# Where matmul operands begin in SBUF: two groups of tiles moved by 96 and 64 bytes

## The chip, the cores and the metric

The kernel runs on one core of a Trainium2 chip. The metric is the device time of one execution in microseconds (us): 1058.58 us, the median of three runs (1058.28 to 1059.94), before the change. A core has TensorE (PE; its weight loads are shown apart as PEld), VectorE (DVE), ScalarE (ACT), GpSimd (POOL) and SyncE (SP), which work side by side and wait for each other by semaphores. SBUF is the on-chip memory; a tile takes the same range of bytes in each of 128 partitions, so "address" here means the byte offset in a partition, and "phase" means that offset modulo 256.

## The reference

One layer of an encoder block on a stream of 1040 rows (16 learned meta rows and 1024 of the input) and 1024 columns, all in float32:

```python
u = rms_norm(h, pre_w)
rq, rk, rv, rg, aq, ak, av, ag, gr, ga = split(u @ w_in)
y_r = (group_norm(retention_fwd(rq, rk, rv) + retention_bwd(rq, rk, rv)) * ret_nw * silu(rg)) @ w_rb
y_a = (windowed_sink_attention(aq, ak, av) * silu(ag)) @ w_ab
out = (sigmoid(gr) * y_r + sigmoid(ga) * y_a) @ w_o
return h + rms_norm(out, post_w)          # meta rows dropped
```

Retention has 4 heads and chunks of 128 rows; attention has 8 query heads, 2 key heads, and sees 128 rows to either side, the meta rows and a sink.

## The kernel before

**Precision.** Each float32 operand of a matmul is split into a high part in the type float32r and the low rest, and a product is three matmuls, in `mm3` (lines 74 to 76): high by high, low by high, high by low. In `nc.tensor.matmul(o, ah, bh)` the second argument is the stationary operand, loaded as weights (128 x 128), and the third is the moving one, whose columns (mostly 512 or 256) stream past. Lines 74 and 75 move the same high part past two sets of weights, line 76 moves the low part. ScalarE or GpSimd makes the high part (`pool_hi`, line 87), VectorE the low one (`dve_lo`, line 90).

**Stages.** Up to about 26 us the input is loaded, scaled and split into `big`, four tiles of 4 x 1040 columns that stay in place; the rows of each are 4160 bytes long. Up to 290 us follow the four retention heads (`retention`), up to 580 us attention (`attention`), both with projections between them (`proj` with `big` as the moving operand, `projT` with `big` as the stationary one). From there on come four products in the manner of Strassen's method (`Phase`, named z for the gates, r and a for the two branches, o for the output): the weight blocks are summed and split into stationary operands `lh` and `ll`, and the right operands are either quarters of the stream, kept in the tiles `big`, or sums of quarters, `T1` in `big` and `T2`, `T3`, `T4` in tiles of their own ("T" in the groups of the profile). Each product is four rows k of `mm3` with 512 columns. The order of the instructions on each engine comes from a planner that works on the program as it is written, with some orders given by hand (`follow`, `issue_after`).

**Where tiles lie.** Tile pools are stacked in SBUF from the left (from low addresses up) or from the right (`side="right"`, from the top down); SBUF is full to within 32 bytes. The right-hand pools are `wp` (weights `wh`, `wl`, and `xm`), `aw` (split queries `aqh`, `aql`, and `raw`), and, in the place of `aw` and `wp` once attention is done, `lp` (`lh`, `ll`, raw weights, sums). The pools on the left are `keep` (small vectors first, then `big`), `ra`, the retention's and attention's own, and in their place at the end `yp`, `gp`, and `yt`, which holds `T2` to `T4`. The program as built places them so:

| tiles | role in matmuls | phase before |
|---|---|---|
| `big`, row k of 4 | moving, in `projT` stationary | 0, 64, 128, 192, by row and column |
| `T2`, `T3`, `T4` | moving | 64 |
| `lh`, `ll`, `wh`, `wl`, `weh`, `aqh` | stationary (`wh`, `wl` moving in `projT`) | 224 |
| retention's and attention's own operands | both | 192 |

The lines that the change touches: `nsink` (line 94, the negated sink logits, read in attention), `mhalf` (line 99, a vector of -0.5, the exponent of `pow` on GpSimd in lines 382, 602 and 1297), and `ms1` in `square` (line 1290 on), a column of 4 bytes per block of output rows, one of four buffers in the pool `gp`, below `yt`.

Of the kernel before, what the change touches and what calls it, by code (L numbers as in the profile page):

```python
# [7 lines left out]
F32 = mybir.dt.float32  # L8
# [8 lines left out]
P = 128  # L17
# [21 lines left out]
def block_kernel(ctx: ExitStack, tc: tile.TileContext, x0, xT, x, meta, w_in, w_rb, w_ab, w_out, post_w,  # L39
# [2 lines left out]
    PSUM = bass.MemoryType.PSUM  # L42

    keep = ctx.enter_context(tc.tile_pool(name="keep", bufs=1))
    w_stack = ExitStack()
    wp = w_stack.enter_context(tc.tile_pool(name="wp", bufs=1, side="right"))
    ps = ctx.enter_context(tc.tile_pool(name="ps", bufs=1, reuse_waits="tile", space=PSUM))
# [43 lines left out]


    vec = keep.tile([P, 2 * KT], F32, name="vec")
    nsink = keep.tile([P, 8], F32, name="nsink")
    dtab = keep.tile([P, 28], F32, name="dtab")
    rcol = keep.tile([P, 9], F32, name="rcol")
    rbc = keep.tile([P, T], F32, name="rbc")
    rnw = keep.tile([P, KT], F32, name="rnw")
    mhalf = keep.tile([P, 16], F32, name="mhalf")
    nc.vector.memset(mhalf, -0.5)  # L100

    def fetch_w(src, u):
# [163 lines left out]
    with tc.tile_pool(name="setup", bufs=1, reuse_waits="tile") as st:  # L266
# [89 lines left out]
        for c in range(9):  # L356
            a, b = cols(c)
            t = st.tile([P, D if c < 7 else T], F32, tag="xn" if c < 7 else "xr", bufs=7 if c < 7 else KT - 1,
                        name=f"xn{c}")[:, 0:D]
# [553 lines left out]
    def gtile(name):  # L913
        return gp.tile([P, 512], F32, tag="g", bufs=6, name=name)
# [347 lines left out]
    def o_post(u, i, j, o, to=None):  # L1262
        if not rows:
            o_head()
        r = 2 * (u ^ 2) + i
        s = slice(512 * j, 512 * j + 512)
        if r not in rows:
            rows[r] = (gp.tile([P, 3], F32, tag="ms2", bufs=4, name=f"ms2_{r}"), [], [])
            if u == 3:
                xres[i] = (lp if i else keep).tile([P, 4, 256], F32, tag="wr", bufs=2, name=f"xres{i}")  # L1270
                xres[i] = xres[i].rearrange("p a b -> p (a b)")
                nc.sync.dma_start(xres[i], x[P * r:P * r + P])
        m2, parts, _ = rows[r]
        square(r, m2, j, o)
        to = o if to is None else to
        if u == 3:

            if not i:
                nc.vector.tensor_tensor(to, o, pw[:, s], mul)
            o = xres[i]  # L1280
        parts.append((s, to, o))
        if len(parts) == 2:
            o_out(r)

    def square(r, m2, c, o):
        m1 = rows[r][2]
        jk = gtile(f"jk{r}_{c}")
        nc.scalar.activation(jk[:, 0:o.shape[1]], o, AF.Square, accum_out=m2[:, c:c + 1])
        if not m1:
            m1.append(gp.tile([P, 1], F32, tag="ms1", bufs=4, name=f"ms1_{r}"))  # L1290
            nc.vector.tensor_scalar(m1[0], m2[:, c:c + 1], 0.25 / D, EPS, op0=ALU.mult, op1=ALU.add)
        else:
            nc.vector.scalar_tensor_tensor(m1[0], m2[:, c:c + 1], 0.25 / D, m1[0], op0=ALU.mult, op1=ALU.add)
# [12 lines left out]
    def o_tail(o, a):  # L1306
        m2, parts, _ = rows[3]
        s = slice(a, a + 256)
        square(3, m2, 2 * (a // 256), o[:, s])
        scaled = nc.vector.tensor_tensor(o[:, s], o[:, s], pw[:, s], mul).ins  # L1310
        if a:
            with tc.issue_after(scaled):
                for c, t, _ in parts:
                    nc.vector.tensor_tensor(t, t, pw[:, c], mul)  # L1314
            parts.append((slice(0, 512), o, xres[1]))
            o_out(3)
# [229 lines left out]
    yp, gp, yt = (ctx.enter_context(tc.tile_pool(name=n, bufs=1, reuse_waits="tile")) for n in ("yp", "gp", "yt"))  # L1546
# [84 lines left out]
```

## Time and profile before

| | |
|---|---|
| median of three runs | 1058.58 us (1058.28 to 1059.94) |
| profiled execution, first to last instruction | 1057.8 us |
| TensorE busy | 1047.6 us, 5880 matmuls |
| weight loads busy | 906.6 us |
| VectorE, ScalarE, GpSimd busy | 839.3, 507.2, 229.0 us |
| moved by DMA | 188.43 MB |

The profiled execution's span is 0.8 us below the median of the runs: that much lies around it. Matmuls are pipelined: the duration that the profile gives of one (about 395 ns at 512 columns) overlaps the next, so the busy share of TensorE says only that it has work; how fast it goes is read from start to start. In rows that list single instructions the columns are start and duration in us, engine, line, operation, names of out<-in, rows * columns of the array and the form.

### The profile page before, as it was taken

What the parts mean: (1) busy time and instruction counts of PE and PEld (TensorE: products, weight loads), DVE (VectorE), ACT (ScalarE), POOL (GpSimd) and SP (SyncE); (2) the same over time, 40 slices, a digit from 0 to 9 for tenths busy, and PEclk for the clock granted to TensorE, in tenths of its full rate; (3) what the DMA queues carried; (4) which work ended last, traced back from release to release, by engine and by line L of the source; (5) the groups of instructions that cost most, each with busy time, mean ns of one, the idle gap of its engine ahead of it and who ended that gap; (6) DMA issues with size and microseconds to landing.
All of it is one profiled execution on the core that took longest, in us unless ns stands there. A gap on an engine that the chain in (4) does not pass through costs nothing. (4 is left out here: it accounts for less than half of the span.)

```text
span 1057.8 us, 17223 instructions
## 1 busy us (share of the span) xinstructions
PE 1047.6 (99%) x5880; PEld 906.6 (86%) x5880; DVE 839.3 (79%) x1788; ACT 507.2 (48%) x1127; POOL 229.0 (22%) x338
## 2 busy tenths in 40 slices
PE   9999999999999999999999999999999999999997
PEld 8998999989989888988888888787888888788886
DVE  7876758768875777778769988998799799778665
ACT  5531422523524566655667554455556446334432
POOL 3345244243242332444310000000000000111032
PEclk9999999999999999999999999999999999999999
DMA  9433222242231466665549679999925746789463
GB/s 352 168 86 86 70 42 80 71 98 89 84 83 61 101 181 192 165 181 159 165 155 338 201 254 321 302 309 353 387 94 168 250 159 232 225 226 317 119 120 79
DMA packets 96758, 188.43 MB, mean 178 GB/s; under 512 B 10944, under 2 KB 35552, under 8 KB 95856
## 3 DMA queue, kind: packets, MB, share of 16 engines
q1 hardware_dynamic: 79120, 162.89, 45.6%
q0 software_dynamic: 10176, 14.73, 9.2%
q10 hardware_dynamic: 7376, 9.73, 2.6%
q8 instruction: 46, 0.75, 0.3%
q14 instruction: 40, 0.33, 0.1%
HBM read 124.32 MB, written 57.68 MB: 172 GB/s over the span
## 5 line engine op out<-in xcount | busy, mean ns | idle before, releaser
L1246 POOL DMA_DIRECT2D mx_d<-c1a x4 | 3.6, 891 | 401.6 <-DVE c1a L1237 382.4
L75 PE MATMUL bz<-T,llz 128*128 128x512 f32 x192 | 75.9, 395 | 0.0
L76 PE MATMUL bz<-T,lhz 128*128 128x512 f32 x192 | 75.7, 394 | 0.0
L74 PE MATMUL bz<-T,lhz 128*128 128x512 f32 x192 | 75.6, 396 | 0.0
L74 PE MATMUL pv<-wh,big 128*128 128x256 f32 x256 | 73.3, 286 | 0.0
L75 PE MATMUL pv<-wh,big 128*128 128x256 f32 x256 | 73.3, 286 | 0.0
L76 PE MATMUL pv<-wl,big 128*128 128x256 f32 x256 | 73.2, 286 | 0.0
L75 PE MATMUL bz<-big,llz 128*128 128x512 f32 x176 | 69.6, 395 | 0.2 <-DVE llz L90 0.2
L76 PE MATMUL bz<-big,lhz 128*128 128x512 f32 x176 | 69.5, 395 | 0.0
L74 PE MATMUL bz<-big,lhz 128*128 128x512 f32 x176 | 68.7, 395 | 0.5 <-ACT lhz L942 0.5
L1377 ACT ACTIVATE p<-raw,nm 128x401 f32<-128x401 f32 (+1 forms) x64 | 38.4, 601 | 33.7 <-DVE nm L1374 32.4
L1387 POOL TENSOR_SCALAR p<-p,den 128x400 f32<-128x400 f32 (+1 forms) x60 | 37.8, 687 | 68.2 <-DVE den L1380 64.1
L74 PE MATMUL paq<-big,wh 128*128 128x512 f32 x128 | 51.8, 405 | 0.0
L75 PE MATMUL paq<-big,wl 128*128 128x512 f32 x128 | 50.7, 396 | 0.0
L76 PE MATMUL paq<-big,wh 128*128 128x512 f32 x128 | 50.5, 395 | 0.0
L75 PEld LDWEIGHTS pv<-wh,big 128*128 128x128 f32 x256 | 48.3, 189 | 0.4
L74 PEld LDWEIGHTS pv<-wh,big 128*128 128x128 f32 x256 | 48.2, 188 | 0.4
L76 PEld LDWEIGHTS pv<-wl,big 128*128 128x128 f32 x256 | 48.3, 189 | 0.3
L76 PEld LDWEIGHTS bz<-T,lhz 128*128 128x128 f32 x192 | 36.0, 188 | 8.9
L75 PEld LDWEIGHTS bz<-T,llz 128*128 128x128 f32 x192 | 36.0, 188 | 8.8 <-DVE llz L90 0.3
L74 PEld LDWEIGHTS bz<-T,lhz 128*128 128x128 f32 x192 | 36.0, 188 | 8.7
L90 DVE TENSOR_TENSOR wl<-wr,wh 128x1024 fp32r<-128x1024 f32 x28 | 34.8, 1247 | 10.8 <-POOL wh L87 6.7
(616 smaller groups left out, 3613.6 us busy)
## 6 DMA issues: line engine op xcount, KB each, us to landing
wrz<-in_w_in_dram SPq DMA_DIRECT2D x32, 512.0 KB, 6.2
wr<-in_w_in_dram SPq DMA_DIRECT2D x29, 512.0 KB, 4.0
we<-in_w_in_dram SPq DMA_DIRECT2D x16, 512.0 KB, 4.2
tg<-tg_d SPq DMA_DIRECT2D x32, 256.0 KB, 5.0
T<-preT SPq DMA_DIRECT2D x6, 1024.0 KB, 8.2
e<-e ACTq DMA_DIRECT2D x20, 256.0 KB, 2.6
e<-e SPq DMA_DIRECT2D x20, 256.0 KB, 4.6
xn<-in_x_dram SPq DMA_DIRECT2D x8, 512.0 KB, 9.2
```

Of the source, the lines that this page charges most:

```text
L74: nc.tensor.matmul(o, ah, bh, start=first, stop=False, **kw)
L75: nc.tensor.matmul(o, al, bh, start=False, stop=False, **kw)
L76: latest[:] = [nc.tensor.matmul(o, ah, bl, start=False, stop=last, **kw).ins]
L90: return nc.vector.tensor_tensor(o, i, hi.bitcast(F32), ALU.subtract).ins
L1246: nc.gpsimd.dma_start(d, to, accum_op=ALU.add)
L1377: last["exp"] = nc.scalar.activation(p[:, 0:1 + wid], raw[e_][:, 0:1 + wid], AF.Exp, scale=-1.0, bias=nm_[:, e_:e_ + 1], accum_out=den[:, ...
L1387: nc.gpsimd.tensor_scalar(pt[e_][:, 0:wid], pt[e_][:, 0:wid], den[:, e_:e_ + 1], 1.0, op0=ALU.mult, op1=ALU.mult)
```

## The change

`nsink` leaves the left-hand pool `keep` for a new right-hand pool `edge`, opened before all others on that side, where it takes 24 columns (96 bytes) of which 8 are used: all other right-hand tiles move down by 96 bytes. `mhalf` grows from 16 to 24 columns, which gives back the 32 bytes that `nsink` took, so that `big` and all behind it stay where they were; four small vectors ahead of it (and `mhalf` itself) move by 32 bytes. `ms1` gets six buffers instead of four, each of which takes 32 bytes: `yt` behind it moves up by 64 bytes. In the program as built, the phase of `T2` to `T4` goes from 64 to 128 and that of `wh`, `wl`, `weh`, `xm`, `aqh`, `aql`, `lh`, `ll`, and the other tiles of `lp` from 224 to 128; `raw` goes from 32 and 128 to 192 and 32. `big` and the operands of retention and attention in left-hand pools keep their addresses. The instructions on every engine and their order are the same; one wait of GpSimd in front of the last `pow` on an `ms1` is gone, and the fill of `mhalf` is longer.

```diff
     keep = ctx.enter_context(tc.tile_pool(name="keep", bufs=1))
+    edge = ctx.enter_context(tc.tile_pool(name="edge", bufs=1, side="right"))
     w_stack = ExitStack()
...
-    nsink = keep.tile([P, 8], F32, name="nsink")
+    nsink = edge.tile([P, 24], F32, name="nsink")[:, 0:8]
...
-    mhalf = keep.tile([P, 16], F32, name="mhalf")
+    mhalf = keep.tile([P, 24], F32, name="mhalf")
     nc.vector.memset(mhalf, -0.5)
...
         if not m1:
-            m1.append(gp.tile([P, 1], F32, tag="ms1", bufs=4, name=f"ms1_{r}"))
+            m1.append(gp.tile([P, 1], F32, tag="ms1", bufs=6, name=f"ms1_{r}"))
```

## The prediction

> **What bounds the kernel.** I read the page first, then the busy time by stage, then the waits of TensorE, and last single matmuls in order of time.
>
> ```profile
> span 1057.8 us, 17223 instructions
> ...
> PE 1047.6 (99%) x5880; PEld 906.6 (86%) x5880; DVE 839.3 (79%) x1788; ACT 507.2 (48%) x1127; POOL 229.0 (22%) x338
> ...
> PEclk9999999999999999999999999999999999999999
> ...
> DVE u3o L1300 0%; DVEq L1627 0%; DVE c5o L1314 0%
> ```
>
> The chain that ended last is not followed back far enough to say anything. The busy shares do: TensorE is at 99% for the whole span, at an undiminished clock. The stages (us, then busy time and count per engine) say it more sharply:
>
> ```profile
> 700.00:870.00 170.00, 170.00 (x731) 136.77 (x730) 152.25 (x250) 90.59 (x161) 0.00 (x0) 1.00 0.70 244
> ...
> 965.00:1057.80 92.80, 86.24 (x383) 69.91 (x381) 60.01 (x112) 34.92 (x74) 18.18 (x22) 0.99 0.54 138
> ```
>
> From 700 to 870 us TensorE has no gap at all; 729 matmuls of 512 columns begin there (two of the 731 began before), 170.00 / 729 = 233.2 ns from start to start. In the last stage only the tail behind the last matmul is without TensorE work (92.80 - 86.24 = 6.6 us). So the time is a number of matmuls times the interval between their starts. The waits of TensorE agree; these are the two longest:
>
> ```profile
> PE idle L309 <- DVE warm L207: 1.5, 1, 1.5
> PE bz L74 <- ACT lhz L942: 0.5, 1, 0.5
> ```
>
> After the 1.5 us at the start nothing that the trace shows keeps TensorE waiting for more than 0.5 us. What a matmul saves, the kernel saves; what it loses, the kernel loses.
>
> **Do the intervals hang on addresses?** The rows of `big` are 4160 bytes long, 64 more than a multiple of 256, so the four rows k of one product start at four different phases (byte address modulo 256). Here is one product from `big` (start, busy, engine, line, tiles), the first of the three matmuls of each k:
>
> ```profile
> 782.48 0.39 PE L74 MATMUL bz<-big,lhz 128*128 128x512 f32 x1
> ...
> 783.17 0.40 PE L74 MATMUL bz<-big,lhz 128*128 128x512 f32 x1
> ...
> 783.88 0.39 PE L74 MATMUL bz<-big,lhz 128*128 128x512 f32 x1
> ...
> 784.57 0.39 PE L74 MATMUL bz<-big,lhz 128*128 128x512 f32 x1
> ...
> 785.27 0.39 PE L74 MATMUL bz<-big,lhz 128*128 128x512 f32 x1
> ```
>
> The moving operand starts at phase 128, 192, 0 and 64 in turn, and three matmuls take 0.69, 0.71, 0.69 and 0.70 us. Two products on a summed block `T`, always at phase 64:
>
> ```profile
> 788.05 0.40 PE L74 MATMUL bz<-T,lhz 128*128 128x512 f32 x1
> 788.29 0.39 PE L75 MATMUL bz<-T,llz 128*128 128x512 f32 x1
> ...
> 793.42 0.39 PE L76 MATMUL bz<-T,lhz 128*128 128x512 f32 x1
> 793.65 0.39 PE L74 MATMUL bz<-big,lhz 128*128 128x512 f32 x1
> ```
>
> 24 matmuls in 5.60 us: 233.3 ns each, 0.700 us for three. Taking the differences of successive starts over the whole trace (those under 250 ns, so that waits are out), with the stationary operand at phase 224, gives for `big`: 232.0 ns at phase 0 (466 intervals), 232.4 at 64 (457), 231.4 at 128 (457), 234.5 at 192 (466); for `T`: 233.4 (992). Where these lie, by the answers on the tile `big` (minimum, median and maximum of one duration, first and last start), its two largest groups of first matmuls with 512 columns:
>
> ```profile
> L74 PE MATMUL bz<-big,lhz x176: 391/394/497, 556.7 to 818.6; 128*128 128x512 f32 x176
> ...
> L74 PE MATMUL paq<-big,wh x128: 388/394/484, 292.9 to 505.0; 128*128 128x512 f32 x128
> ```
>
> and of the tile `T`:
>
> ```profile
> L74 PE MATMUL bz<-T,lhz x192: 389/396/402, 580.3 to 810.2; 128*128 128x512 f32 x192
> ...
> L74 PE MATMUL bo<-T,lho x52: 279/394/403, 978.4 to 1050.7; 128*128 128x512 f32 x44, 128*128 128x256 f32 x8
> ...
> L74 PE MATMUL br<-T,lhr x48: 392/394/403, 827.2 to 888.5; 128*128 128x512 f32 x48
> ...
> L74 PE MATMUL ba<-T,lha x48: 394/396/402, 905.5 to 972.3; 128*128 128x512 f32 x48
> ```
>
> So phase 128 is the cheapest of the four for the moving operand, and the dearest is only 3.1 ns above it.
>
> **The change part by part.** No instruction is added, removed or reordered on any engine; only addresses differ, a fill is 24 columns instead of 16, and one wait on GpSimd is dropped.
>
> *1. Moving operand of the T products, 64 to 128.* From the rows above, (192 + 48 + 48 + 44) x 3 = 996 matmuls of 512 columns. The same step within `big` saves 232.4 - 231.4 = 1.0 ns; from T's own 233.4 to 231.4 it would be 2.0. I take the middle, 1.5 ns, since T shares with the row at 64 the phase and differs in repeating it: 996 x 1.5 = -1.5 us. Ends: 2.0 ns saved (-2.0 us), or 1.1 lost, if 128 beside the new stationary phase costs what the row at 192 costs, 234.5 (+1.1 us).
>
> *2. Stationary operand, 224 to 128.* Phase 224 is 32 bytes off a multiple of 64, 128 is not. The trace has few 512-column intervals in which the weights for the next matmul lie at a multiple of 64: where such a matmul stands ahead of retention or attention. The first and the last of 39:
>
> ```profile
> 81.59 0.39 PE L76 MATMUL pq<-big,wh 128*128 128x512 f32 x1
> 81.83 0.28 PE L74 MATMUL pa<-vh,sh 128*128 128x256 f32 x1
> ...
> 560.21 0.40 PE L74 MATMUL bz<-big,lhz 128*128 128x512 f32 x1
> 560.44 0.28 PE L76 MATMUL po<-pal,vah 128*128 128x256 f32 x1
> ```
>
> Their means are 231.1 (moving phase 0, 8 intervals), 231.8 (64, 16), 232.8 (128, 8) and 233.3 (192, 7): against the means above -0.9, -0.6, +1.4 and -1.2 ns, together -0.3. I take that for all matmuls of 512 columns whose stationary operand moves, 996 with `T` and 1920 with `big`: to the groups of 176 and 128 above come, among the groups by shape,
>
> ```profile
> L74 PE MATMUL pe<-big,weh 128*128 128x512 f32 x80 | 32.0, 404 | 0.0
> ...
> L74 PE MATMUL bo<-big,lho 128*128 128x512 f32 x64 | 25.2, 394 | 0.0
> L74 PE MATMUL br<-big,lhr 128*128 128x512 f32 x64 | 24.9, 394 | 0.0
> L74 PE MATMUL ba<-big,lha 128*128 128x512 f32 x64 | 24.9, 394 | 0.0
> ...
> L74 PE MATMUL pq<-big,wh 128*128 128x512 f32 x48 | 19.0, 395 | 0.0
> ...
> L74 PE MATMUL pq<-big,w 128*128 128x512 f32 x16 | 6.7, 430 | 0.1
> ```
>
> which makes 640 groups of three. 2916 x -0.3 = -0.9 us. Ends are the two extremes: -1.2 ns, so -3.5 us, and +1.4 ns, so +4.1 us. This is the widest term, from the thinnest rows.
>
> [...]
>
> *3. Matmuls of 256 columns.* In projT the moving weights go from 224 to 128 (960 matmuls), in proj the stationary ones (432). The trace has all pairings but the old one with both off 64: moving off and stationary on a multiple of 64 118.7 ns (900 intervals), the reverse 118.4 (486), both on it 118.5 (679). These lie within 0.3 ns: 960 x -0.1 + 432 x 0.1, about -0.1 us. Ends +-0.4 us (1392 x 0.3).
>
> *4. The rest.*
>
> ```profile
> 0.80 0.07 DVE L100 MEMSET mhalf<- 128x16 f32 x1 [0.80 <-PEq L1621]
> ```
>
> is the fill in order of time, and of the line that uses `ms1`:
>
> ```profile
> L1297 POOL TENSOR_TENSOR ms<-ms,mhalf x8: 560/739/1542, 1005.8 to 1052.7; 128x1 f32<-128x1 f32 x8
> ...
>   DVE ms L1293: 54.0, 6
> ```
>
> The longer fill costs between nothing and 0.04 us (half of 0.07 more), ahead of the warm-up matmuls that TensorE waits 1.5 us for and that no result needs: zero. The wait dropped on GpSimd is on one of four `ms1` buffers used again; GpSimd stands idle there until VectorE has made the value (54.0 us in six waits), so a buffer freed earlier ends nothing: zero. VectorE, ScalarE and DMAs write the moved tiles; were they slower by an address, TensorE's waits above leave them room.
>
> Sum: -1.5 - 0.9 - 0.1 = -2.5 us. The profiled execution has a span of 1057.8 us, 0.8 below the median of the runs, 1058.58; the terms are intervals inside the span, so I take them from the median: 1056.1 us. The ends: -2.0 - 3.5 - 0.4 = -5.9, 1052.7 us; +1.1 + 4.1 + 0.4 = +5.6, 1064.2 us.
>
> **The rivals.**
>
> *No change.* A T product never changes phase: row k+1 of T and its low half begin at the same phase, so each matmul ends and begins alike, and 0.700 us for three may be a step that the repetition sets, not phase 64. Then moving T gives nothing, and with weights that do not matter the time is 1058.6 us. For it: whichever buffers hold the weights, T gives 0.700, while products on `big`, which step through the phases, give 0.69 to 0.71. Against it: the means by phase in `big`. [...] I include in this case the sum without term 2, 1057.0.
>
> *Slower: both streams at one phase.* After the change, weights and moving rows begin at the same byte modulo 256 in the 996 T products and in a quarter of those on `big` (480). If reading both from one place in turn costs what the worst phase costs over the best, 234.5 - 231.4 = 3.1 ns, that is 1476 x 3.1 = +4.6 us, less the 1.5 of term 1: 1061.7 us. It decides once equal phases cost more than 1.7 ns (2.5 us / 1476). For it: the means at 512 columns differ with the distance between the two phases and never show distance 0 for long. Against it: retention and attention have both operands at phase 192 throughout, and those 256-column intervals are among the 679 at 118.5, no dearer than the rest.
>
> **How the numbers follow.** About 0.2% (2.1 us) is what a measurement of this kernel can tell from no change. My forecast, -2.5 us, gets 0.43; it includes the gains down to 1052.7. No change, from 1056.5 to 1060.7, gets 0.30: half of the terms would have to fail. Slower gets 0.27, since term 2 may as well be positive and equal phases are new here. The range runs from 1052.5 to 1063.0, the ends less what the chances leave out above; the forecast's own is 1052.5 to 1056.5.
>
> **What would show it.** Right: the same counts in every group, the span 2 to 3 us shorter, T triples at 0.694 to 0.696 us instead of 0.700 (24 matmuls in 5.56 instead of 5.60), and the products on `big` 0.3 ns per matmul shorter. Term 1 is wrong if 24 T matmuls still take 5.60 us; the slower rival holds if they take 5.65 or more. Term 2 shows in `big` alone: twelve matmuls took 785.27 - 782.48 = 2.79 us. What makes the whole wrong is an interval that hangs on the two phases jointly in a way that phase 224 never let the trace show.

## The result, and the profile after

The changed kernel takes 1054.05 us (median of six runs, 1052.91 to 1056.54) against 1058.43 us before (six runs): a ratio of 0.9959, with a 95% interval of 0.9949 to 0.9969, or 4.4 us less. Lines after 45 are one higher than before, because a line is added. The page of the changed kernel, in the lines that answer to those shown of before:

```profile
span 1051.7 us, 17222 instructions
...
PE 1040.9 (99%) x5880; PEld 905.4 (86%) x5880; DVE 838.3 (80%) x1788; ACT 506.5 (48%) x1127; POOL 228.4 (22%) x338
...
DVE u3o L1301 0%; DVEq L1628 0%; DVE c5o L1315 0%
```

The same 5880 matmuls, TensorE at 99% as before, the busy time of the weight loads and of the other engines unchanged within 1.2 us. The same stretch of time holds more matmuls, 734 where there were 731 (us; busy time and count of PE, PEld, DVE, ACT, POOL; clock; DMA share; GB/s):

```profile
700.00:870.00 170.00, 169.37 (x734) 137.28 (x733) 153.41 (x253) 91.98 (x165) 0.00 (x0) 1.00 0.69 241
```

Where the time went is seen in single matmuls. First the 24 matmuls of two products on a summed block, before (start, busy, engine, line, operation, tiles): from the first to the first of the next two products.

```profile
799.23 0.40 PE L74 MATMUL bz<-T,lhz 128*128 128x512 f32 x1
...
804.83 0.40 PE L74 MATMUL bz<-T,lhz 128*128 128x512 f32 x1
```

The same two products after the change:

```profile
794.85 0.39 PE L75 MATMUL bz<-T,lhz 128*128 128x512 f32 x1
...
800.31 0.39 PE L75 MATMUL bz<-T,lhz 128*128 128x512 f32 x1
```

5.60 us before, 5.46 after: 233.3 and 227.5 ns per matmul. One product on `big` after the change, the first matmul of each of its four rows:

```profile
778.26 0.39 PE L75 MATMUL bz<-big,lhz 128*128 128x512 f32 x1
...
778.95 0.40 PE L75 MATMUL bz<-big,lhz 128*128 128x512 f32 x1
...
779.64 0.40 PE L75 MATMUL bz<-big,lhz 128*128 128x512 f32 x1
...
780.34 0.39 PE L75 MATMUL bz<-big,lhz 128*128 128x512 f32 x1
...
781.04 0.39 PE L75 MATMUL bz<-big,lhz 128*128 128x512 f32 x1
```

2.78 us, where the same product took 2.79 in the prediction. Summing all start-to-start intervals of the two traces by what the first matmul moves, the 996 on `T` fall from 232.8 to 228.1 us, those on `big` with 512 columns stay at 450.9 and 451.0, the 256-column ones fall by 0.9, all others by 0.6. The spans of the two profiled executions are 6.1 us apart, more than the medians, since single executions scatter: that of after took 1053.81 us in all, 2.1 more than its span. About 2 us lie around every span on record, not the 0.8 us between the span and the median of before, so the profiled execution of before, at about 1059.9 us, would be the longest of its three. The forecast is a sum of differences and does not hang on this. On `T` the interval, with those of 250 ns and more left out as in the prediction, falls alike in the four products, from 233.4 to 233.6 ns to 227.6 to 227.7; that the 0.9 and 0.6 us on other matmuls are scatter is likely, but not shown.

### The profile page after: what moved, and what is told of

Same layout as the page of the kernel before. It is cut to its first block, busy times and chain, and to the rows that moved or that the text cites. A ratio compares the mean times of both kernels' runs of the same rounds, so it can differ in the third digit from the quotient of the medians.

```text
span 1051.7 us, 17222 instructions
## 1 busy us (share of the span) xinstructions
PE 1040.9 (99%) x5880; PEld 905.4 (86%) x5880; DVE 838.3 (80%) x1788; ACT 506.5 (48%) x1127; POOL 228.4 (22%) x338
```

## Experiments

Three theories were tested. *Distance*: an interval shrinks to about 227 ns when moving and stationary operand begin at the same phase and successive matmuls repeat it. *Phase 128*: the moving operand's own phase decides, which is term 1 of the prediction. *Multiple of 64*: the stationary operand's phase decides, which is the idea behind term 2. Kernels are named by the phases of `T` and of the right-hand pools, so that before is T64 R224 and the change T128 R128.

### One half of the change alone: T128 R224

```diff
-            m1.append(gp.tile([P, 1], F32, tag="ms1", bufs=4, name=f"ms1_{r}"))
+            m1.append(gp.tile([P, 1], F32, tag="ms1", bufs=6, name=f"ms1_{r}"))
```

> Only ms1 gets six buffers: T2 to T4 begin at phase 128, the stationary operands stay at 224 (32 bytes off a multiple of 64). Theory 'distance' (an interval falls to about 226.7 ns when moving and stationary operand begin at the same phase and the product repeats it): distance 96, so three T matmuls do not reach 0.680 us, they stay at 0.69 to 0.70, and the kernel at 1056.5 to 1059. Theory 'phase 128' (the moving operand's phase alone, as term 1 of the prediction has it): three T matmuls at 0.680 us, kernel at about 1054. Theory 'multiple of 64' (the stationary operand's phase alone): no change of T, 0.700 us, 1058.4.

Measured: 1060.12 us, ratio 1.0010 (1.0001 to 1.0019). The same two products:

```profile
799.16 0.39 PE L74 MATMUL bz<-T,lhz 128*128 128x512 f32 x1
...
804.78 0.39 PE L74 MATMUL bz<-T,lhz 128*128 128x512 f32 x1
```

5.62 us, no better than before; over all of `T` 234.0 ns per matmul (995 intervals). Theory *phase 128* falls. The other two stand, though the kernel is 1.1 us slower than *distance* had allowed.

### The other half alone: T64 R128

```diff
+    edge = ctx.enter_context(tc.tile_pool(name="edge", bufs=1, side="right"))
...
-    nsink = keep.tile([P, 8], F32, name="nsink")
+    nsink = edge.tile([P, 24], F32, name="nsink")[:, 0:8]
...
-    mhalf = keep.tile([P, 16], F32, name="mhalf")
+    mhalf = keep.tile([P, 24], F32, name="mhalf")
```

> Only the right-hand pools move, stationary operands at phase 128, T2 to T4 stay at 64. Theory 'distance': phases 64 apart, no 0.680 us, kernel at 1057 to 1059.5. Theory 'phase 128': T unchanged at 0.700 us, 1058. Theory 'multiple of 64': three T matmuls at 0.680 us, about 1054.

Measured: 1056.83 us, ratio 0.9983 (0.9974 to 0.9993).

```profile
796.12 0.39 PE L75 MATMUL bz<-T,lhz 128*128 128x512 f32 x1
...
801.72 0.39 PE L75 MATMUL bz<-T,lhz 128*128 128x512 f32 x1
```

`T` stays at 5.60 us, so a stationary operand on a multiple of 64 does not shorten it either. The kernel still gains 1.8 us by the ratio, just below what *distance* had expected, and T96 R128 and T64 R192 below, with other unequal phases and weights on a multiple of 64, gain about 1.2 each. In the profiled execution the sum on `big` is 1.5 us lower than before (449.4 us), and those on the matmuls of 256, 128 and 400 columns 0.6 each. Whether one to two microseconds belong to the weights' phase alone stays open: with `big` and the weights at the same phases as here, the sum on `big` is 451.0 us in the change and 449.6 in T96 R128, so single executions differ by as much.

### Equal phases that are neither 128 nor a multiple of 64: T224 R224

```diff
-            m1.append(gp.tile([P, 1], F32, tag="ms1", bufs=4, name=f"ms1_{r}"))
+            m1.append(gp.tile([P, 1], F32, tag="ms1", bufs=9, name=f"ms1_{r}"))
```

> ms1 gets nine buffers and nothing else is changed: T2 to T4 begin at phase 224, as the stationary operands do; neither is at 128 nor at a multiple of 64. Theory 'distance': three T matmuls at 0.680 us, the kernel as fast as with the change, about 1054. Theory 'phase 128' and theory 'multiple of 64': no gain, 0.70 us or more, 1058 or more.

Measured: 1054.87 us, ratio 0.9962 (0.9947 to 0.9977), as good as the change itself.

```profile
795.72 0.39 PE L74 MATMUL bz<-T,lhz 128*128 128x512 f32 x1
...
801.20 0.39 PE L74 MATMUL bz<-T,lhz 128*128 128x512 f32 x1
```

5.48 us, 0.685 for three matmuls. Here nothing on the right-hand side is moved, and `T` begins 32 bytes off a multiple of 64. Only *distance* had expected it.

### Equal phases at 64: T64 R64

The change with `edge` 40 columns wide and `ms1` at four buffers:

```diff
-    nsink = edge.tile([P, 24], F32, name="nsink")[:, 0:8]
+    nsink = edge.tile([P, 40], F32, name="nsink")[:, 0:8]
...
-            m1.append(gp.tile([P, 1], F32, tag="ms1", bufs=6, name=f"ms1_{r}"))
+            m1.append(gp.tile([P, 1], F32, tag="ms1", bufs=4, name=f"ms1_{r}"))
```

> The new right-hand tile is 160 bytes instead of 96 and ms1 keeps four buffers: both operands of the T products begin at phase 64. Theory 'distance': 0.680 us for three, about 1054. Theory 'phase 128': T unchanged at 0.700 us, 1058. Theory 'multiple of 64': 0.680 us, about 1054.

Measured: 1053.24 us, ratio 0.9948 (0.9933 to 0.9963).

```profile
794.76 0.40 PE L75 MATMUL bz<-T,lhz 128*128 128x512 f32 x1
...
800.21 0.39 PE L75 MATMUL bz<-T,lhz 128*128 128x512 f32 x1
```

5.45 us with `T` exactly where it was before: it never needed to move. (The right-hand pools lie 160 bytes lower throughout, so before the change more was free than the 32 bytes given above.)

### How near is equal: T96 R128 and T64 R192

The change with five `ms1` buffers (32 bytes apart), and with `edge` 8 columns wide and `ms1` at four buffers (128 bytes apart):

```diff
-            m1.append(gp.tile([P, 1], F32, tag="ms1", bufs=6, name=f"ms1_{r}"))
+            m1.append(gp.tile([P, 1], F32, tag="ms1", bufs=5, name=f"ms1_{r}"))
```

```diff
-    nsink = edge.tile([P, 24], F32, name="nsink")[:, 0:8]
+    nsink = edge.tile([P, 8], F32, name="nsink")[:, 0:8]
...
-            m1.append(gp.tile([P, 1], F32, tag="ms1", bufs=6, name=f"ms1_{r}"))
+            m1.append(gp.tile([P, 1], F32, tag="ms1", bufs=4, name=f"ms1_{r}"))
```

> The change with five ms1 buffers instead of six: T begins at phase 96, stationary operands at 128, 32 bytes apart. If only equal phases count, T falls back to 233 to 234 ns per matmul and the kernel to 1058 to 1059; if being near is enough, T stays near 227 to 229 ns and the kernel near 1054.

> The new right-hand tile is 32 bytes and ms1 keeps four buffers: T begins at phase 64, stationary operands at 192, 128 bytes apart. If the distance counts modulo 256 (or more), T stays at 233 to 234 ns and the kernel at 1057.5 to 1059; if it counts modulo 128, T takes 227 to 228 ns and the kernel about 1054.

Measured: 1057.52 us, 0.9989 (0.9979 to 1.0000), and 1057.51 us, 0.9988 (0.9977 to 0.9998). The two products on `T` in the first,

```profile
796.73 0.40 PE L75 MATMUL bz<-T,lhz 128*128 128x512 f32 x1
...
802.33 0.40 PE L75 MATMUL bz<-T,lhz 128*128 128x512 f32 x1
```

and in the second:

```profile
795.82 0.39 PE L75 MATMUL bz<-T,lhz 128*128 128x512 f32 x1
...
801.39 0.40 PE L75 MATMUL bz<-T,lhz 128*128 128x512 f32 x1
```

5.60 and 5.57 us. 32 bytes apart is not near enough, and 128 apart is not equal; its mean of 232.2 ns is a little below the 233 to 234 expected. In every unequal case the stationary phase was the higher one. All distances tried on `T`, with the mean interval over the whole trace:

| kernel | phases of T, R | apart | ns per matmul on T | ratio of times |
|---|---|---|---|---|
| T64 R64 | 64, 64 | 0 | 227.4 | 0.9948 |
| the change | 128, 128 | 0 | 227.6 | 0.9959 |
| T224 R224 | 224, 224 | 0 | 228.4 | 0.9962 |
| T96 R128 | 96, 128 | 32 | 233.1 | 0.9989 |
| T64 R128 | 64, 128 | 64 | 233.3 | 0.9983 |
| T128 R224 | 128, 224 | 96 | 234.0 | 1.0010 |
| T64 R192 | 64, 192 | 128 | 232.2 | 0.9988 |
| before | 64, 224 | 160 | 233.4 | 1 |

### Equal phases in every row of `big` too

The rows of `big` begin at four phases because they are 4160 bytes long. Padding them to 4352 bytes puts all of them at 128, beside stationary operands at 128. That takes 3 KB, for which some pools get fewer buffers; the control has those alone, and both have the same order of instructions on every engine. (The planner's order for the control differs from that of the change in 126 of the 5880 places on TensorE.) The edits of the control against the change, and then of the padded kernel against the control:

```diff
-            t = st.tile([P, D if c < 7 else T], F32, tag="xn" if c < 7 else "xr", bufs=7 if c < 7 else KT - 1,
+            t = st.tile([P, D if c < 6 else T], F32, tag="xn" if c < 6 else "xr", bufs=6 if c < 6 else KT - 1,
...
-        vmeta = rp.tile([NM, 256], F32, tag="vmeta", bufs=2, name=f"vmeta{h}")
+        vmeta = rp.tile([NM, 256], F32, tag="vmeta", bufs=1, name=f"vmeta{h}")
...
-                sd = rp.tile([P, P], F32, tag="sd", bufs=3, name=f"sd{h}_{c}")
+                sd = rp.tile([P, P], F32, tag="sd", bufs=2, name=f"sd{h}_{c}")
...
-        return (yp if j else lp).tile([P, 512], dt, tag=f"sg{int(j)}", bufs=8 if j else 7, name=name)
+        return (yp if j else lp).tile([P, 512], dt, tag=f"sg{int(j)}", bufs=7 if j else 6, name=name)
```

```diff
-    big = [[keep.tile([P, 4, T], R, name=f"big{i}_{s}") for i in range(2)] for s in range(2)]
+    big = [[keep.tile([P, 4, 1088], R, name=f"big{i}_{s}") for i in range(2)] for s in range(2)]
```

> Control for the next run: the changed kernel with fewer buffers (xn six, vmeta one, sd two, the stage tiles six and seven), which makes room and moves nothing else in phase. Both the theory 'distance' and a theory that only T can gain expect what the fewer buffers cost: 1054 to 1057, T at 227 to 228 ns, big at 232 to 233 ns on average.

> As the control, and the rows of big are padded to 1088 columns, so that all four rows of every product begin at phase 128 (all 1920 matmuls of 512 columns on big, both operands at 128); the order of the instructions is the control's. Theory 'distance': big falls from 232 to 233 ns to 227 to 228 ns, 1920 x 5 = 9.6 us less than the control, 1044 to 1047. If the gain of T is special to T (its rows lie whole tiles apart), big stays above 231 ns and the kernel within 2 us of the control.

Measured: the control 1053.03 us, 0.9946 (0.9932 to 0.9961), so the fewer buffers cost nothing, against the 1054 to 1057 expected; padded 1046.86 us, 0.9883 (0.9866 to 0.9899). Two products on `big` in the control, from the first matmul to the first of the next product,

```profile
778.25 0.39 PE L75 MATMUL bz<-big,lhz 128*128 128x512 f32 x1
...
783.81 0.39 PE L75 MATMUL bz<-T,lhz 128*128 128x512 f32 x1
```

and in the padded kernel, with the rows of the first of them:

```profile
776.75 0.39 PE L75 MATMUL bz<-big,lhz 128*128 128x512 f32 x1
...
777.43 0.39 PE L75 MATMUL bz<-big,lhz 128*128 128x512 f32 x1
...
778.11 0.39 PE L75 MATMUL bz<-big,lhz 128*128 128x512 f32 x1
...
778.79 0.39 PE L75 MATMUL bz<-big,lhz 128*128 128x512 f32 x1
...
782.19 0.39 PE L75 MATMUL bz<-T,lhz 128*128 128x512 f32 x1
```

5.56 us become 5.44, 0.68 us for every three matmuls, in each row alike. Over the trace an interval on `big` is 227.6 ns (1845 intervals) where the control has 233.4, 233.1, 229.8 and 232.8 at phases 0, 64, 128 and 192. So the gain is not special to `T`. All 512-column matmuls on `big` together take 8.2 us less than in the control; the medians are 6.2 us apart, short of the 9.6 expected. Most of what is missing can be seen in the two traces: the 256-column intervals go from 118.2 to 118.9 ns (2047 each), 1.3 us in sum with their waits, and `T` loses 0.9 us to waits. One of 1.2 us is new among the waits of TensorE:

```profile
PE idle L310 <- DVE warm L208: 1.5, 1, 1.5
PE bz L75 <- ACT u2z L1025: 1.2, 1, 1.2
```

The padded kernel is the fastest of all: 11.7 us below the runs of before on the same chip, 2.7 times the gain of the change.

## Why the prediction was right, and where it was not

The forecast of 1056.1 us was 2.0 us too high; the sign and the range hold. The reason given for it does not, so that the number came out near is luck: of its two main terms the first has the wrong cause, and the second was added as if it worked by itself. The prediction did name what would make the whole wrong, an interval that hangs on the two phases jointly in a way that phase 224 never let the trace show. That is what the runs show. Alone, the move of `T` costs 1.1 us (0.1 to 2.0) and the move of the weights gains 1.8 (0.7 to 2.8), by the ratios; together they gain 4.4 (3.3 to 5.4).

*What bounds the kernel* was right: with an unchanged order of instructions, the time moved with the sum of the intervals, and padding `big` took 8.2 us out of the TensorE stream, of which 6.2 reached the end.

*Term 1* (moving operand of `T`, -1.5 us) named the right 996 matmuls, and these took 4.7 us less in the change. But its step from the phases of `big` to `T` failed. It read phase 128 as the cheapest phase of the moving operand; T128 R224 is that step alone, and gives no gain at all (234.0 ns against 233.4). What 128 had in the change was company: the weights began there too. The means by phase came from one execution, and their order does not hold in another: T128 R224 and T224 R224 leave `big` and the weights where they were, and over 43 products on `big` in the four `Phase`s whose twelve matmuls stand together, the row at 64 takes 0.2 ns less than the row at 128 in the first and 1.1 more in the second (1.8 more before). Nor was any distance among those means zero: 128 and 64 beside 224 are 96 and 160 apart. The seven intervals at 192 beside 192 (233.3 ns) were single ones.

*Term 2* (stationary operand, -0.9 us) is neither borne out nor refuted as it stands. Terms 2 and 3 alone make the kernel T64 R128, whose 1.8 us (0.7 to 2.8) include the forecast of 1.0; but nothing of it lies on `T`, and on `big` the term is smaller than what single executions differ by (450.9 and 451.0 us before and in the change, 449.4 in T64 R128). What failed is the form: for `T` its weight cannot be given apart from term 1, since either move alone shortens nothing there and both together take off 4.7 us. Adding the two as independent terms was the mistake.

The sum without term 2, 1057.0 us, would have the stationary phase not count. In the runs it counts: under one and the same moving phase of 128, `T` takes 234.0 ns with weights at 224 (T128 R224) and 227.6 with weights at 128 (the change). That `T` gave 0.700 us whichever buffers held the weights could not test it, since all these buffers began at 224.

*Term 3* (256 columns, -0.1 us) moved by -0.9 us between the two profiled executions, which are single ones. *The rest* at zero held: the waits of TensorE after the change begin with these:

```profile
PE idle L310 <- DVE warm L208: 1.5, 1, 1.5
PE bz L75 <- ACT lhz L943: 0.5, 1, 0.5
PE br L76 <- DVE llr L91: 0.4, 1, 0.4
```

The first two stood there before; the third, of 0.4 us, is new.

*The rivals.* "Slower: both streams at one phase" named what matters, equal phases, with the sign reversed: it priced them at 3.1 ns more per matmul, and they took 5.8 less on `T`. The row that decided against it, retention and attention at 192 beside 192 being no dearer, was about 256 columns, where equality neither helped nor cost much (118.2 ns in the control, 118.9 padded). "No change" took the 0.700 us for a step that repetition sets. At unequal phases nothing bears that out: `T` repeats its phases and takes 232.2 to 234.0 ns, `big` steps through four and takes 232.5 on average before. At equal phases repetition does count: 229.2 to 230.9 ns in a single equal row, 226.7 to 226.8 where equal rows follow each other (below).

## What to carry to other kernels

Where TensorE is the bound and a kernel streams 512 float32r columns per weight load, let the moving and the stationary operand begin at the same byte modulo 256, and keep that so from one matmul to the next: it was worth 2.5% of such a matmul on `T` here (233.4 ns to 227.6), for 96 and 64 bytes, and 3 KB of padding brought the like to `big` (227.6 ns where the control has 229.8 to 233.4). Look at start-to-start intervals, not at durations (0.39 to 0.40 us before and after) or busy time (99% both times), and group them by the phases of both operands jointly; a table by one operand's phase alone misled. When two moves may act only together, run each alone before believing a sum of the two.

## What the runs showed that was not expected

Where a product on `T` repeats equal phases, a matmul of 512 columns takes 227.4 to 228.4 ns on average; at every other distance that was tried on `T` (32, 64, 96, 128 and 160 bytes) 232.2 to 234.0, with no slope in between. The absolute phase matters little (64, 128 and 224 lie within 1.0 ns). The period is neither 64 nor 128 bytes (233.3 and 232.2 ns at these distances). In the padded kernel half of the intervals on `big` have operands 256 bytes apart modulo 512, and they take the same (227.7 ns, 923 intervals, and 227.6 ns, 922), so it is not 512 either. At 256 columns equality gave nothing, 118.9 ns against 118.2 in the control.

Equal phases in one row are not enough; the neighbours count. With the weights at 128, 64 or 192, one of the four rows of every product on `big` is equal, and over the same 43 products as above it is the cheapest of the four each time, but at 229.2, 230.0 and 230.9 ns (the change, T64 R64, T64 R192), where the other three rows take 232.0 to 233.5. In the change this does not even show in the sum on `big`. On `T`, the four rows of the 52 products whose twelve matmuls stand together take 228.0, 228.1, 226.8 and 226.7 ns in the change and 229.0, 228.1, 227.8 and 226.7 in T224 R224: the interval comes down as the product repeats. In the padded kernel, where the product ahead mostly has equal phases too, every row on `big` and on `T` takes 226.7 to 226.8.

Why the two addresses act together in this way, and why equality gained nothing at 256 columns, no run here shows.
